# Sums through HBM at the turn between two passes, a gate chain moved to the last pairs, and a shorter head of the mix

## The chip, the core and the metric

The kernel runs on one core of one Trainium2 chip. The metric is the device time of one execution in microseconds (us). Five engines work side by side, each with a queue of its own: PE (matmuls; it adds up in eight banks), DVE and ACT (element-wise work and evacuation of the banks), POOL, and SP, which issues the DMAs in the order in which they are written. HBM is the memory outside the core.

## The reference

One layer of a hybrid encoder over a prompt of 2048 tokens and a sample of 64, width 1024:

```
mod = c @ w_mod + b_mod; shift, scale, gate = split(mod, 3)
h = rmsnorm(x, norm_in_w) * (1 + scale) + shift
b_gate, c_gate, h_a, g_a, z, xbc_raw, dt_raw = split(h @ w_in)
u = c_gate * h_a
y_a = gated_rmsnorm(b_gate * causal_dwconv(u), g_a)
x, B, C = split(silu(causal_dwconv(xbc_raw)))
y = ssd_chunked(x, softplus(dt_raw), a, B, C) + d_skip * x      # the scan over time
y_b = gated_rmsnorm(y, z)
out = rmsnorm(x + gate * (concat(y_a, y_b) @ w_out))
```

Outputs are out for prompt and sample, and the states of the convolutions and of the scan.

## The kernel before

All products are made in pairs of rounded parts: a float32 tensor is split into a rounded high part (ACT casts, `split` L170) and the rest as a low part (DVE subtracts, L171), and a product is three matmuls, high by high, high by low, low by high.

`phase_project` computes h @ w_in by a scheme of seven products instead of eight on 2 × 2 blocks. The second input dimension and the tokens are halved, so the input h of a pass stands as blocks A11, A12, A21, A22, and the seven products read A11, S1, S2, S4, S3, A12, A22, where S1 = A21 + A22, S2 = S1 − A11, S4 = A12 − S2 and S3 = A11 − A21. A *pair* g is two tiles of 128 columns of w_in. Pairs 0 to 27 go over the first pass (tokens 0 to 1023, matmuls 512 wide), pairs 28 to 55 over the second (tokens 1024 to 2111, the sample among them; two units 272 wide). The kinds are z pairs, pairs of x, B and C (`raw_row`), and a pairs in groups of four: c, h, g and b. Pair 22 is an h pair, 25 to 31 are z pairs, 52 to 55 are c, h, g and b.

The main loop goes over pairs 2 to 54 and, in each, over the seven products s. Each step issues, in this order: the matmuls of product (g, s) (`product`, L275); the weights' high part of a later product (`w_hi`, ACT, L241); the hooks that are written down for (g, s); background work that fits (taps of the convolutions, L432); the weights' low part (`w_lo`, DVE, L232, with subtractions of weight quarters in place, `raw<-raw`); and `evac`. `evac` copies products 0, 1 and 2 to `keep` (ACT, L300), adds keep to products 3, 4 and 5 (DVE, L308), and copies product 6 (ACT, L306). Products 0, 2, 4 and 6 accumulate in one bank, 1 and 3 in another. So product 2 can't start before the copy of product 0 to keep is done, and the same holds two products further on each time. Engines run what they got in order, so what stands ahead of an evacuation in the order of the code delays PE.

The input of the second pass is prepared in hooks. Before, x is loaded in two groups of four chunks of 128 rows (pairs 24 to 26), normalized, transposed and stored to `hs_d` in HBM. From pair 27 on, `second_in` loads blocks of it (`t_a`), and seven hooks `second(s)` make the sums (L849 and L232) and their splits, one after each product, into the places that the products of pair 27 have just left. Other hooks: `load_state`, `turn_state`, `sample_x` and `sample_h` for the sample; `gate_load` and `gate_part`, eight parts of the product of c with the gate's third of w_mod. The last part adds b_mod in four quarters (`gb`, L628): SP loads a quarter of b_mod, DVE adds the bank, SP stores it, in turns through one tile.

After pair 54 `last_pair` computes the last pair as plain products into all eight banks (L1146), and prepares the mix meanwhile: `split_wo` splits sixteen tiles of w_out (ACT L1234, DVE L1235) that SP loads as `wo_raw` into tiles that come free (`homes`); `decay` computes the scan's decays of the first chunk (ACT, L1257 and L1258); `evac_last` evacuates the banks (L482). `phase_mix` then goes over 17 chunks; its first matmuls (`sd`, L1295) use banks of the last pair. Its head splits the rest of w_out.

## Time and profile before

| | |
|---|---|
| median of 3 runs | 1800.84 us (1800.67 to 1802.07) |
| profiled execution | 1800.68 us |
| its span, first to last instruction | 1798.9 us |
| mean granted clock of PE | 0.987 |
| PE, DVE, ACT busy | 1721.1, 1308.4, 824.8 us |
| HBM read, written | 158.74, 49.69 MB |

The profile is of one execution. An instruction's row gives its start from the beginning of the span, its duration, engine, line and operation, out<-in, how many were grouped (x), and in brackets the idle time of its engine before it and what ended it. Rows of groups end with the busy time, the mean ns of one, and the idle time before. "PEclk" is the clock that PE was granted, 1.00 being full speed.

### The profile page before, as it was taken

Reading aid. Unit: us, or ns where it says so; the run is one execution under the profiler, and the core shown is the slowest. Engines: PE = TensorE matmul, PEld = TensorE weight load, DVE = VectorE, ACT = ScalarE, POOL = GpSimd, SP = SyncE. Lnnn points to the kernel's source line nnn. Section 1 sums busy time; section 2 is a strip of 40 time slices with the busy share of each in tenths; the row PEclk is TensorE's granted clock in tenths of the full one; section 3 lists DMA queues with packets and bytes.
Section 4 is the critical chain, followed back from the end, with each engine's and each line's share of the span. In section 5 each row is a group of like instructions: output and inputs, shape, how many; then the busy total and the mean of one; then the engine's idle time right before and its main releaser. Section 6 shows DMA issues by size and latency. Waiting matters only on the chain.

```text
span 1798.9 us, 26916 instructions
## 1 busy us (share of the span) xinstructions
PE 1721.1 (96%) x10561; PEld 1512.7 (84%) x10561; DVE 1308.4 (73%) x2015; ACT 824.8 (46%) x1559; POOL 101.8 (6%) x222
## 2 busy tenths in 40 slices
...
GB/s 333 70 88 76 96 104 82 95 118 78 110 129 186 195 109 85 100 73 73 80 103 89 87 78 96 83 84 109 217 146 167 108 173 107 170 111 170 112 147 35
DMA packets 181826, 210.17 MB, mean 117 GB/s; under 512 B 21012, under 2 KB 147972, under 8 KB 181700
## 3 DMA queue, kind: packets, MB, share of 16 engines
...
HBM read 158.74 MB, written 49.69 MB: 116 GB/s over the span
## 4 chain that ended last, share of the span: by engine, by line
PE 83%; DVE 6%; ACT 4%; DMA 4%; issue 2%; SPq 0%; POOL 0%; POOLq 0%; ACTq 0%; DVEq 0%
PE bank L275 53%; PE mm L1398 13%; PE mm L1405 6%; PE sd L1323 2%; PE sd L1327 2%; PE sd L1329 2%; DMA t_a<-hs_d 1%; PE sd L1295 1%; PE sd L1299 1%; PE bank L1025 1%; DMA rb<-r_d 1%; DVE w L232 1%; DVE xt L208 1%; DMA wo_raw<-in_w_out_dram 1%; DMA hs_d<-h_g 1%
## 5 line engine op out<-in xcount | busy, mean ns | idle before, releaser
L275 PE MATMUL bank<-hiS,w 128*128 128x272 f32 (+1 forms) x2560 | 600.9, 324 | 13.9 <-ACT keep L300 13.7
L275 PEld LDWEIGHTS bank<-hiS,w 128*128 128x128 f32 x2560 | 432.7, 189 | 52.7 <-ACT keep L300 18.2
L275 PE MATMUL bank<-hiA,w 128*128 128x272 f32 (+1 forms) x1920 | 452.9, 324 | 20.8 <-DVE z_row L308 9.8
L275 PE MATMUL bank<-loS,w 128*128 128x272 f32 (+1 forms) x1280 | 413.3, 323 | 0.0
L275 PEld LDWEIGHTS bank<-hiA,w 128*128 128x128 f32 x1920 | 325.8, 190 | 50.3 <-DVE z_row L308 10.8
L232 DVE TENSOR_TENSOR w<-raw,w 128x512 fp32r<-128x512 f32 x318 | 217.8, 688 | 173.2 <-ACT w L241 158.8
L241 ACT CAST w<-raw 128x512 fp32r<-128x512 f32 x318 | 196.2, 622 | 255.1 <-PE bank L275 135.3
L275 PE MATMUL bank<-loA,w 128*128 128x272 f32 (+1 forms) x960 | 310.5, 323 | 0.0
L275 PEld LDWEIGHTS bank<-loS,w 128*128 128x128 f32 x1280 | 242.3, 189 | 15.9
L275 PEld LDWEIGHTS bank<-loA,w 128*128 128x128 f32 x960 | 182.0, 190 | 12.2
L300 ACT COPY keep<-bank 128x272 f32<-128x272 f32 (+1 forms) x240 | 106.2, 450 | 137.9 <-PE bank L275 137.4
L381 DVE SCALAR_TENSOR_TENSOR acc<-raw_row,par,acc 128x1024 f32<-128x1024 f32 (+1 forms) x96 | 126.4, 1317 | 2.0
L232 DVE TENSOR_TENSOR raw<-raw 128x512 f32<-128x512 f32 x161 | 111.0, 689 | 3.7
L1398 PE MATMUL mm<-woh,vah 128*128 128x512 f32 (+1 forms) x272 | 109.5, 403 | 0.0
L1398 PE MATMUL mm<-woh,vbh 128*128 128x512 f32 (+1 forms) x272 | 109.2, 401 | 0.0
L1398 PE MATMUL mm<-wol,vah 128*128 128x512 f32 (+1 forms) x272 | 106.5, 392 | 0.0
L1398 PE MATMUL mm<-wol,vbh 128*128 128x512 f32 (+1 forms) x272 | 106.1, 390 | 0.0
L1257 ACT ACTIVATE lt<-rb,acum 128x128 f32<-128x128 f32 x256 | 78.3, 388 | 6.0 <-DMA rb<-r_d 5.2
L1405 PE MATMUL mm<-woh,vbh 128*128 128x512 f32 (+1 forms) x272 | 67.2, 390 | 0.0
L1405 PE MATMUL mm<-woh,vah 128*128 128x512 f32 (+1 forms) x272 | 67.2, 389 | 0.0
L241 ACT CAST w<-t 128x512 fp32r<-128x512 f32 x53 | 32.7, 618 | 75.0 <-PE bank L275 75.0
L1423 ACT ACTIVATE t<-xr 128x512 f32<-128x512 f32 (+1 forms) x34 | 21.5, 632 | 92.8 <-DVE xr L1422 92.8
...
## 6 DMA issues: line engine op xcount, KB each, us to landing
...
```

What stands on the lines that cost most here:

```text
L232: DVE.tensor_tensor(out=out, in0=a, in1=b, op=ALU.subtract)
L241: ACT.copy(out=w[:, 0], in_=w_src(g, j))
L275: PE.matmul(ps[:, 0:n], w[:, a, k, :], h[:, k, o:o + n], start=(s in (0, 1, 5) and k == 0 and i == 0), stop=(k == 3 and i == 2), skip_grou ...
L300: ACT.copy(out=keep[s][:, o:o + n], in_=b["y" if s == 1 else "x"][:, 0:n])
L381: DVE.scalar_tensor_tensor(out=acc[:, 0:n], in0=r[:, k:k + n], scalar=cb_w(k, t), in1=acc[:, 0:n], op0=ALU.mult, op1=ALU.add)
L1257: ACT.activation(out=lt[:, h, :], in_=rb[:, h, :], func=AF.Relu, scale=-1.0, bias=acum[:, c, h0 + h:h0 + h + 1])
L1323: PE.matmul(py4[64 * e:64 * e + 64, j, :], xd[:, 2 * j + e, :], lt[:, 2 * j + e, :], start=True, stop=True)
L1327: PE.matmul(po4[:, j, :], state[:, hf, j * 128:(j + 1) * 128], xb[:, 6 + j // 2, :], start=True, stop=True)
L1329: PE.matmul(ps[:, g * 256:(g + 1) * 256], bc[:, g, :], xe[:, 4 * g:4 * g + 4, :].rearrange("p h q -> p (h q)"), start=True, stop=True)
L1398: PE.matmul(ps[:n], hl[:, 0, k, 0:n], wo[k0 + k][i][:, nn * 512:(nn + 1) * 512], start=(k == 0 and i == 0), stop=False)
L1405: PE.matmul(ps[:n], hl[:, 1, k, 0:n], wo[k0 + k][0][:, nn * 512:(nn + 1) * 512], start=False, stop=(k == 7))
L1423: ACT.activation(out=t[:n], in_=xr[:n, s], func=AF.Square, accum_out=ss[:n, nn:nn + 1])
```

## The change

1. The second pass's input is loaded in four groups of two chunks from pair 19 on; four transposes of 128 × 128, two per input tile, go to one bank ahead of its two copies. In pairs 23 to 25 the blocks are loaded (`h_q`), the eight adds are made there, and the four sums are stored to a new tensor `hq_d` in HBM. From pair 26 on the inputs of the products are loaded ready made (`t_q`), three ahead, and pairs 27 and 28 only split them; for products 2 and 3 the splits are written behind the evacuation of their step (`behind`).
2. State and sample hooks go from pairs 22 and 23 to 18 and 19, the gate's parts from pairs 18 to 22 to pairs 51 to 53.
3. In `last_pair` the banks are numbered anew, the first chunk's decays are loaded straight into their tiles and computed behind the first two weight splits, nine splits of w_out are made rather than twelve, and the evacuations stand behind the sixth and the ninth. The head of the mix splits seven rather than four.

DVE around the middle of pair 27, where the splits of S4 and S3 stand (`w2` to `w4` are weight parts of pair 28, `z_row` evacuations; the order of before first):

```order
L232 TENSOR_TENSOR w2_4675<-raw_4400,w2_4675 128x512
L308 TENSOR_TENSOR z_row_4644<-bank2_4602,keep2_4661 128x512
L232 TENSOR_TENSOR t_a21_4591<-t_a12_4649,t_a21_4591 128x1088
L232 TENSOR_TENSOR t_a21_4593<-t_a12_4651,t_a21_4593 128x1088
L171 TENSOR_TENSOR loS4_4704<-t_a21_4591,hiS4_4703 128x1088
L171 TENSOR_TENSOR loS4_4704<-t_a21_4593,hiS4_4703 128x1088
L232 TENSOR_TENSOR w3_4699<-raw_4400,w3_4699 128x512
L308 TENSOR_TENSOR z_row_4644<-bank1_4570,keep1_4629 128x512
L232 TENSOR_TENSOR t_a11_4587<-t_a11_4587,t_a21_4728 128x1088
```

```order
L233 TENSOR_TENSOR w2_4674<-raw_4473,w2_4674 128x512
L309 TENSOR_TENSOR z_row_4645<-bank2_4599,keep2_4660 128x512
L233 TENSOR_TENSOR w3_4690<-raw_4473,w3_4690 128x512
L309 TENSOR_TENSOR z_row_4645<-bank1_4579,keep1_4630 128x512
L172 TENSOR_TENSOR loS2_4695<-t_q_4503,hiS2_4694 128x1088
L172 TENSOR_TENSOR loS2_4695<-t_q_4505,hiS2_4694 128x1088
L233 TENSOR_TENSOR w4_4719<-t3_4627,w4_4719 128x512
L309 TENSOR_TENSOR z_row_4644<-bank3_4704,keep0_4597 128x512
L172 TENSOR_TENSOR loS4_4724<-t_q_4622,hiS4_4723 128x1088
L172 TENSOR_TENSOR loS4_4724<-t_q_4624,hiS4_4723 128x1088
```

Between the evacuations of z_row stood two adds and two splits; now the first two evacuations have only a weight part between them, and the third stands ahead of the splits of S4.

DVE at the end of pair 53, an h pair (`u_row` its evacuations, L432 and L433 taps, `w5` and `w6` weight parts of pair 54, `raw` the subtraction that ACT's cast for `w6` reads):

```order
L232 TENSOR_TENSOR w4_11136<-t3_11008,w4_11136 128x512
L308 TENSOR_TENSOR u_row_11038<-bank2_11110,keep0_10974 128x272
L308 TENSOR_TENSOR u_row_11038<-bank3_11111,keep0_10974 128x272
L432 SCALAR_TENSOR_TENSOR c_row_10816<-u_row_11041,par_70,c_row_10816 128x1090
L232 TENSOR_TENSOR w5_11171<-raw_10780,w5_11171 128x512
L232 TENSOR_TENSOR raw_10780<-raw_10780 128x4x128
L418 TENSOR_TENSOR u_row_11038<-u_row_11038,c_row_10815 128x1024
L420 TENSOR_TENSOR u_row_11038<-u_row_11038,c_row_10815 128x64
```

```order
L233 TENSOR_TENSOR w4_11174<-t3_11036,w4_11174 128x512
L309 TENSOR_TENSOR u_row_11066<-bank2_11148,keep0_11000 128x272
L309 TENSOR_TENSOR u_row_11066<-bank3_11149,keep0_11000 128x272
L629 TENSOR_TENSOR gb_11215<-bank5_10711,gb_11215 2x256 x4
L433 SCALAR_TENSOR_TENSOR c_row_10824<-u_row_11069,par_71,c_row_10824 128x1090
L233 TENSOR_TENSOR w5_11209<-raw_10784,w5_11209 128x512
L233 TENSOR_TENSOR raw_10784<-raw_10784 128x4x128
L419 TENSOR_TENSOR u_row_11066<-u_row_11066,c_row_10823 128x1024
```

The gate's four adds now stand ahead of the tap, the weight part and the subtraction. Before, they stood in pair 22 in the like place.

ACT in the last pair (`woh` high parts of w_out, `lt` the decays):

```order
L1234 ACTIVATE woh0_11627<-wo_raw_11659,par_70 128x1024
L1234 ACTIVATE woh1_11629<-wo_raw_11661,par_70 128x1024
L1234 ACTIVATE woh2_11631<-wo_raw_11663,par_70 128x1024
L1234 ACTIVATE woh3_11633<-wo_raw_11621,par_70 128x1024
L1234 ACTIVATE woh4_11635<-wo_raw_11622,par_70 128x1024
L1257 ACTIVATE lt_11683<-rb_11619,acum_78 128x128 x8
L1258 ACT_TABLE_LOAD
L1258 ACTIVATE lt_11683<-lt_11683 128x1024
L1234 ACTIVATE woh5_11637<-wo_raw_11669,par_70 128x1024
L1234 ACTIVATE woh6_11657<-wo_raw_11673,par_70 128x1024
L1257 ACTIVATE lt_11706<-rb_11695,acum_78 128x128 x8
L1258 ACTIVATE lt_11706<-lt_11706 128x1024
```

```order
L1266 ACTIVATE woh0_11680<-wo_raw_11712,par_71 128x1024
L1187 ACTIVATE lt_11672<-lt_11672,acum_79 128x128 x8
L1189 ACT_TABLE_LOAD
L1189 ACTIVATE lt_11672<-lt_11672 128x1024
L1266 ACTIVATE woh1_11682<-wo_raw_11715,par_71 128x1024
L1187 ACTIVATE lt_11673<-lt_11673,acum_79 128x128 x8
L1189 ACTIVATE lt_11673<-lt_11673 128x1024
L1266 ACTIVATE woh2_11684<-wo_raw_11718,par_71 128x1024
L1266 ACTIVATE woh3_11686<-wo_raw_11720,par_71 128x1024
L1266 ACTIVATE woh4_11688<-wo_raw_11727,par_71 128x1024
L1266 ACTIVATE woh5_11690<-wo_raw_11740,par_71 128x1024
L1266 ACTIVATE woh6_11710<-wo_raw_11753,par_71 128x1024
```

The two decays went from behind the fifth and seventh cast to behind the first and second.

The diff, cut:

```diff
+    hq_d = dram.tile([4, 128, 4, 544], F32, tag="hq_d", name="hq_d")
...
+        def hook_at(t, fn):
+            hook(t // 7, t % 7, fn)
+
         for k in range(8):
-            hook(18 + k // 2, 1 + 3 * (k % 2), lambda k=k: gate_load(k, 2 + k % 2))
-            hook(18 + k // 2 + (k % 2), 6 if k % 2 == 0 else 2, lambda k=k: gate_part(k))
+            hook_at(51 * 7 + 3 + 2 * k, lambda k=k: gate_load(k, 2 + k % 2))
+            hook_at(51 * 7 + 6 + 2 * k, lambda k=k: gate_part(k))
...
-        hook(22, 3, load_state)
-        hook(23, 1, turn_state)
+        hook(18, 6, load_state)
+        hook(19, 3, turn_state)
...
-        hook(22, 5, sample_x)
-        hook(23, 0, lambda: x_scale(xin["s"], xin["ss"]))
-        hook(23, 2, sample_h)
+        hook(18, 0, sample_x)
+        hook(18, 4, lambda: x_scale(xin["s"], xin["ss"]))
+        hook(18, 6, sample_h)
 
         def group_load(gi):
-            xin[gi] = load_rows(range(8 + 4 * gi, 12 + 4 * gi), range(2, 6))
+            xin[gi] = load_rows(range(8 + 2 * gi, 10 + 2 * gi), (2, 3))
             xin[gi, "ss"] = x_ss()
 
         def group_turn(gi, j):
...
-            o = row(6 + j % 2, [128, 2, 512], "h_g")
+            o = row(4 + j, [128, 4, 256], "h_g")
+            for i in range(0, 4, 2):
+                pt = bank()
+                for e in range(2):
+                    k = 4 * j + i + e
+                    for off, n, t in xin[gi]:
+                        PE.transpose(pt[:, 256 * e + off:256 * e + off + n], t[:n, k * 128:(k + 1) * 128], ident[:n, :n])
+                for e in range(2):
+                    k = 4 * j + i + e
+                    ACT.activation(out=o[:, i + e, :], in_=pt[:, 256 * e:256 * e + 256], func=AF.Identity,
+                                   scale=scol[:, k, 0:1], bias=bcol[:, k, 0:1])
+            store_h(o, 4 * j, 256 * gi, 256)
+        for gi in range(4):
+            t0 = 19 * 7 + 1 + 8 * gi
+            hook_at(t0, lambda gi=gi: group_load(gi))
             for i in range(2):
-                k = 2 * j + i
-                pt = turn_x(xin[gi], k)
-                ACT.activation(out=o[:, i, :], in_=pt, func=AF.Identity, scale=scol[:, k, 0:1], bias=bcol[:, k, 0:1])
-            store_h(o, 2 * j, 512 * gi, 512)
-
-        for gi, (gl, gt) in enumerate(((24 * 7, 25 * 7), (25 * 7 + 4, 26 * 7 + 3))):
-            hook(gl // 7, gl % 7, lambda gi=gi: group_load(gi))
+                hook_at(t0 + 3 + i, lambda gi=gi, i=i: x_sums(xin[gi], xin[gi, "ss"], i, i + 1))
+            hook_at(t0 + 5, lambda gi=gi: x_scale(xin[gi], xin[gi, "ss"]))
+            for j in range(2):
+                hook_at(t0 + 6 + 2 * j, lambda gi=gi, j=j: group_turn(gi, j))
+
+
+        blocks = {}
+
+        def sums_in(i):
+            for n, (k0, o) in enumerate(((0, 0), (0, 544), (4, 0), (4, 544))):
+                t = row(2 + n, [128, 2, 544], "h_q")
+                SP.dma_start(out=t, in_=hs_d[:, k0 + 2 * i:k0 + 2 * i + 2, o:o + 544])
+                blocks[n] = t
+
+        def sums_step(i, n):
+            a11, a21, a12, a22 = (blocks[x] for x in range(4))
+            out, x, y, op = ((a22, a21, a22, ALU.add), (a21, a11, a21, ALU.subtract),
+                             (a11, a22, a11, ALU.subtract), (a12, a12, a11, ALU.subtract))[n]
+            DVE.tensor_tensor(out=out, in0=x, in1=y, op=op)
+            SP.dma_start(out=hq_d[n, :, 2 * i:2 * i + 2, :], in_=out)
+
+        for i, t0 in enumerate((23 * 7 + 6, 24 * 7 + 5)):
+            hook_at(t0, lambda i=i: sums_in(i))
+            for n in range(4):
+                hook_at(t0 + 3 + n, lambda i=i, n=n: sums_step(i, n))
+
+        tm = {}
+        SOURCE = {"A11": (hs_d, 0, 0), "A12": (hs_d, 4, 0), "A22": (hs_d, 4, 544),
+                  "S1": (hq_d[0], 0, 0), "S3": (hq_d[1], 0, 0), "S2": (hq_d[2], 0, 0), "S4": (hq_d[3], 0, 0)}
+
+        def second_in(j, r):
+            src, k0, o = SOURCE[PRODS[j]]
+            tm[j] = []
             for i in range(2):
-                hook((gt - 3 + i) // 7, (gt - 3 + i) % 7, lambda gi=gi, i=i: x_sums(xin[gi], xin[gi, "ss"], 2 * i, 2 * i + 2))
-            hook((gt - 1) // 7, (gt - 1) % 7, lambda gi=gi: x_scale(xin[gi], xin[gi, "ss"]))
-            for j in range(4):
-                hook((gt + j) // 7, (gt + j) % 7, lambda gi=gi, j=j: group_turn(gi, j))
-
-        def temp(r, name, k0, o):
-            ts = []
-            for i in range(2):
-                t = row(r + i, [128, 2, 544], name)
-                SP.dma_start(out=t, in_=hs_d[:, k0 + 2 * i:k0 + 2 * i + 2, o:o + 544])
-                ts.append(t)
-            return ts
-
-        tm = {}
-
-        def second_in():
...
-        def second(s):
-            a, b, c = tm["a"], tm["b"], tm.get("c")
-            if s == 1:
-                for i in range(2):
-                    DVE.tensor_tensor(out=b[i], in0=b[i], in1=c[i], op=ALU.add)
-                tm["c"] = temp(6, "t_a12", 4, 0)
...
-            q = PRODS[s]
-            put(q, {"A11": tm["a"], "S1": b, "S2": b, "S4": b, "S3": a, "A12": c, "A22": tm["b"]}[q])
-
-        hook(27, 0, second_in)
-        for s in range(7):
-            hook((27 * 7 + s + 1) // 7, (s + 1) % 7, lambda s=s: second(s))
+                t = row(r + i, [128, 2, 544], "t_q")
+                SP.dma_start(out=t, in_=src[:, k0 + 2 * i:k0 + 2 * i + 2, o:o + 544])
+                tm[j].append(t)
+
+        def second(j):
+            hi, lo = h_tile(PRODS[j], 544)
+            for i, t in enumerate(tm.pop(j)):
+                split(t, hi[:, 2 * i:2 * i + 2, :], lo[:, 2 * i:2 * i + 2, :])
+            if j + 3 < 7:
+                second_in(j + 3, (6, 2, 4)[j % 3])
+
+        hook(26, 0, lambda: second_in(0, 6))
+        hook(26, 1, lambda: second_in(1, 2))
+        hook(26, 2, lambda: second_in(2, 4))
+        behind = {}
+        for j, t, late in ((0, 1, 0), (1, 2, 0), (2, 4, 1), (3, 5, 1), (4, 6, 0), (5, 7, 0), (6, 9, 0)):
+            if late:
+                behind[27, t] = lambda j=j: second(j)
+            else:
+                hook_at(27 * 7 + t, lambda j=j: second(j))
 
...
-            pss = {(f, h): [bank(2 * (f + 2 * h) + u) for u in range(2)] for h in range(2) for f in range(2)}
+            pss = {fh: [bank(no + u) for u in range(2)] for fh, no in (((0, 1), 4), ((1, 1), 2), ((0, 0), 0), ((1, 0), 6))}
...
+            fast = [p1.tile([128, 8, 128], F32, tag="lt", name="lt", bufs=2) for _ in range(2)]
+            p1.tile([128, 8, 128], F32, tag="rb", name="rb_")
+            xbs = [p1.tile([128, 8, 128], F32, tag="xb", name="xb", bufs=2) for _ in range(2)]
...
-            homes = ["w6", "row6", "row7", None, None, "w6", "row6", "row7", "w6", "row6", "row7", "w6"]
+            homes = ["w6", "rb", "row6", "row7", "w6", "rb", "row6", "row7", "w6"]
...
+            def load_decay(hf):
+                SP.dma_start(out=fast[hf], in_=r_d[hf * 8:hf * 8 + 8, :].partition_broadcast(128))
+
+            def decay_first(hf):
+                for h in range(8):
+                    ACT.activation(out=fast[hf][:, h, :], in_=fast[hf][:, h, :], func=AF.Relu, scale=-1.0,
+                                   bias=acum[:, 0, 8 * hf + h:8 * hf + h + 1])
+                ACT.activation(out=fast[hf], in_=fast[hf], func=AF.Exp, scale=-1.0)
+                held[0, hf] = fast[hf]
...
-            for k in range(5):
-                load_o(k)
-            for k in range(12):
+            load_o(0)
+            load_decay(0)
+            load_o(1)
+            load_decay(1)
+            load_o(2)
+            load_o(3)
+            for hf in range(2):
+                SP.dma_start(out=xbs[hf], in_=xb_d[0, :, hf])
+                loads[0, hf] = [xbs[hf], None]
+            SP.dma_start(out=va[:, 0:6, :], in_=va_d[16, :, 0:6, 0:NS_TOK])
+            for k in range(9):
                 split_wo(k, raw_o.pop(k))
-                if k + 5 < 8 or 5 <= k <= 8:
-                    load_o(k + 5 if k < 3 else k + 3)
-                if k == 4:
-                    decay(0, 0)
-                    prefetch(0, 1)
-                    SP.dma_start(out=va[:, 0:6, :], in_=va_d[16, :, 0:6, 0:NS_TOK])
-                if k == 6:
-                    decay(0, 1)
-                if k == 8:
+                if k + 4 < 9:
+                    load_o(k + 4)
+                if k < 2:
+                    decay_first(k)
+                elif k == 5:
                     evac_last(1, True)
                     evac_last(1, False)
             evac_last(0, False)
...
                 evac(p, g, s)
+                if (g, s) in behind:
+                    behind[g, s]()
...
-        for k, tag, bufs in ((12, "xr", 2), (13, "xr", 2), (14, "gate", 1), (15, "nf", 1)):
+
+        def load_o(k, tag, bufs):
             raw_o[k] = sp.tile([128, D], F32, tag=tag, name="wo_raw", bufs=bufs)
             SP.dma_start(out=raw_o[k], in_=w_out[k * 128:(k + 1) * 128, :])
+
+        for k, tag, bufs in ((9, "xr", 2), (10, "xr", 2), (11, "gate", 1), (12, "nf", 1)):
...
-        for k in (12, 13):
+        for k, nxt, tag, bufs in ((9, 13, "xr", 2), (10, 14, "xr", 2), (11, 15, "gate", 1), (12, None, "", 0)):
             split_wo(k, raw_o[k])
+            if nxt:
+                load_o(nxt, tag, bufs)
         join1(0, 0)
         ssd1(0, 1)
         join2(0, 0)
         prefetch(1, 0)
-        for k in (14, 15):
+        for k in (13, 14, 15):
```

25 lines of the change are left out of this document (2 added, 23 removed).

## The prediction, made before the changed kernel was run

> **What bounds the kernel now.** I read the page first, then the waits of PE, then the stretches in which PE stands, and last the rows at their edges.
>
> ```profile
> PE 1721.1 (96%) x10561; PEld 1512.7 (84%) x10561; DVE 1308.4 (73%) x2015; ACT 824.8 (46%) x1559; POOL 101.8 (6%) x222
> ```
>
> PE bounds it, and both kernels issue the same PE work. So the change can only win time in which PE stands (1798.9 − 1721.1 = 77.8 us) or runs at half clock. Who holds PE up:
>
> ```profile
> PE bank L275 <- ACT keep L300: 13.7, 8, 3.5
> PE sd L1295 <- DVE c_row L482: 11.0, 1, 11.0
> PE bank L275 <- DVE z_row L308: 9.8, 3, 6.8
> PE bank L275 <- ACT z_row L306: 7.8, 1, 7.8
> PE bank L275 <- DVE u_row L308: 2.8, 1, 2.8
> ```
>
> (Columns: total us, times, longest.) These are evacuations that come late; nearly all lie at the turn between the passes (pairs 22 to 28) and once at the head of the mix (L1295). The stretches, with PE's busy time first, the granted clock behind POOL, then the DMA's share and GB/s:
>
> ```profile
> 482.50:673.10 190.60, 158.63 (x764) 130.74 (x761) 114.57 (x157) 92.98 (x164) 2.93 (x5) 0.93 0.47 152
> 530.30:599.60 69.30, 66.05 (x317) 53.60 (x316) 37.55 (x58) 42.92 (x84) 2.02 (x2) 1.00 0.52 167
> 599.60:673.10 73.50, 49.49 (x255) 43.10 (x254) 45.75 (x54) 33.39 (x46) 0.00 (x0) 0.84 0.47 156
> 1243.50:1281.30 37.80, 26.79 (x205) 26.57 (x205) 21.72 (x28) 25.28 (x39) 0.00 (x0) 0.87 0.63 210
> ...
> 503.70:507.10 3.40, 3.40 (x10) 2.62 (x9) 3.26 (x5) 1.95 (x5) 0.18 (x1) 0.50 0.04 8
> 521.95:525.35 3.40, 3.40 (x15) 2.81 (x16) 2.23 (x4) 0.98 (x2) 0.00 (x0) 1.00 0.76 214
> 657.30:660.70 3.40, 3.40 (x17) 3.40 (x16) 2.68 (x6) 1.18 (x4) 0.00 (x0) 0.50 0.40 94
> 1271.70:1281.90 10.20, 3.11 (x12) 2.75 (x13) 8.20 (x16) 3.70 (x5) 0.00 (x0) 0.50 0.47 149
> ```
>
> In pairs 22 to 28 (482.5 to 673.1) PE stands 190.60 − 158.63 = 32.0 us, 24.0 of them in pairs 27 and 28 (73.50 − 49.49). The mean clock there is 0.93. Full speed alternates with half speed, so half speed lasts (1 − 0.93) × 2 × 190.6 = 27 us: eight stretches of 3.4 us between the rows 503.70 and 657.30. PE is busy 20.6 us of these, and work at half clock takes twice its time, so 10.3 us are lost. **The ceiling of the turn is 32.0 + 10.3 = 42.3 us.** What brings half clock on:
>
> ```profile
> 502.78 0.50 PE L275 MATMUL bank<-hiA,w 128*128 128x512 f32 x1 [2.83 <-DVE u_row L308]
> 521.95 0.50 PE L275 MATMUL bank<-hiS,w 128*128 128x512 f32 x1 [1.88 <-ACT keep L300]
> 632.87 0.80 PE L275 MATMUL bank<-hiA,w 128*128 128x512 f32 x1 [6.83 <-DVE z_row L308]
> ```
>
> Behind the gap of 2.83 us stands a stretch at 0.50 (503.70), behind that of 1.88 us one at 1.00 (521.95). I count a loss of 1.7 us (half of a busy 3.4) for each new gap of 2.8 us or more, and half of that, 0.8, for one between 1.9 and 2.8. The Trainium skill ("TensorE: Matmul & The Clock Gate", Part 1: The HAM clock gate) has the clock drop when a whole activity window of about 3.4 us was idle. By that rule no gap under 3.4 us costs clock and my sum would come out some 3 us lower; the trace's 2.83 us gap disagrees, and I go by the trace.
>
> **The change, part by part.** *The turn.* Of the old pairs 27 and 28 these rows show what DVE does:
>
> ```profile
> L171 DVE TENSOR_TENSOR loS<-t_a,hiS 128x1088 fp32r<-128x1088 f32 x8 | 10.1, 1289 | 0.0
> L232 DVE TENSOR_TENSOR t_a<-t_a,t_a 128x1088 f32<-128x1088 f32 x6 | 7.6, 1287 | 7.4 <-DMA t_a<-hs_d 7.4
> 629.11 2.49 DVE L171 TENSOR_TENSOR loS<-t_a,hiS 128x1088 fp32r<-128x1088 f32 x2
> 631.52 0.69 DVE L232 TENSOR_TENSOR w<-raw,w 128x512 fp32r<-128x512 f32 x1
> 632.13 0.68 DVE L308 TENSOR_TENSOR z_row<-bank,keep 128x512 f32<-128x512 f32 x1
> 638.85 1.29 DVE L232 TENSOR_TENSOR t_a<-t_a,t_a 128x1088 f32<-128x1088 f32 x1 [6.04 <-DMA t_a<-hs_d]
> ...
> 603.82 0.39 PE L275 MATMUL bank<-hiS,w 128*128 128x512 f32 x1
> 607.67 0.39 PE L275 MATMUL bank<-hiS,w 128*128 128x512 f32 x1
> ```
>
> PE's 6.83 us gap ends with the z_row evacuation of 632.13, which stood behind two adds, two splits and a weight part. After the change the eight adds (8 × 1.29 = 10.3 us) and their DMA waits (7.4 us) are gone from here, and the evacuations of z_row stand ahead of the splits of S2 and S4. What is left between the first split and the last product of pair 27 is 12 splits and, by the order above, 14 weight parts and evacuations. Back to back they take 1.24 and 0.61 (the spacing of rows 629.11 to 632.13): 12 × 1.24 + 14 × 0.61 = 23.4 us. The seven products of pair 27 need 7 × 2.72 = 19.0 (between the last two rows are 17 matmuls in a piece, 3.85 / 17 = 0.2265 each, and a product has twelve). So DVE falls 4.4 us behind, and PE must stand about that long: the lower bound. I walked the queue of each engine by these durations: gaps of 1.4 and 2.25 us at the end of pair 27, and 1.45, 0.45 and 0.95 in pair 28, where ACT's hi casts and DVE's first subtraction of the next weights wait on one another; 6.5 us, and 0.8 of clock. I take 7.3 (4.4 to 14; the upper end adds one more gap like the old one of 6.83).
>
> *The adds in their new place.* The eight adds go to pairs 23 to 25, each between a load of 557 KB from HBM and a store to it. DVE has room: 37.6 busy of 69.3 us in pairs 24 to 26. DMA too, on average: 16 × 0.557 = 8.9 MB more, with what stays some 13 MB in 46 us, or 280 GB/s, where row 521.95 has 214 at a share of 0.76. What is tight is time: a block's load is issued one product after the store of the last turned rows, and its first add stands three products later, 8.2 us. A load like that at 638.85 came 6.0 us after its evacuation. By my walk the loads land 1.3 to 1.8 us ahead of the adds; I take 0.5 us of new stall. Bounds: nothing, or 14 us (at each of two block groups 3.5 to 5.3 us late, with 1.7 of clock). The Trainium skill ("DMA: Bandwidth & Descriptors", Anatomy of one DMA) speaks against these hops: about 2.0 us fixed for each transfer, most of it the receipt of a write, longest into HBM. By its fit a store and the load behind it would take an estimated 6.6 us; that is inside 8.2, so by it the term would be zero, and the sum 0.5 lower.
>
> *State, sample and gate out of pairs 18 to 23.* The state and sample parts go to pairs 18 and 19, where PE stands nowhere now; I count nothing: PE has weights of two pairs loaded as cover; without it one gap like the 2.83 would be the price. The gate's chain leaves pair 22:
>
> ```profile
> 490.93 0.62 PE L620 MATMUL bank<-raw_gate,cvec 128*2 128x256 f32 x8
> 491.62 0.41 DVE L628 TENSOR_TENSOR gb<-bank,gb 2x256 f32<-2x256 f32 x1 [2.80 <-PE bank L620]
> 497.61 0.43 DVE L628 TENSOR_TENSOR gb<-bank,gb 2x256 f32<-2x256 f32 x1 [1.60 <-DMA gb<-in_b_mod_dram]
> 499.45 1.14 ACT L241 CAST w<-raw 128x512 fp32r<-128x512 f32 x2 [7.78 <-DVE raw L232]
> ```
>
> Four adds, each waiting for its own small load, hold DVE from 491.62 to 498.04, three periods of 2.0 us and one add; ACT's cast waits behind for the subtracted weights, 7.78 us, and from that comes the old gap of 2.83 at 502.78 (part of the ceiling). Now the chain stands behind product 6 of pair 53:
>
> ```profile
> 1225.53 0.29 PE L275 MATMUL bank<-hiS,w 128*128 128x272 f32 x1
> 1243.57 0.29 PE L1146 MATMUL bank<-hiS,w 128*128 128x272 f32 x1
> ...
> 1228.67 1.35 DVE L432 SCALAR_TENSOR_TENSOR c_row<-u_row,par,c_row 128x1090 f32<-128x1090 f32 x1
> 1225.28 0.84 ACT L300 COPY keep<-bank 128x272 f32<-128x272 f32 x2
> ```
>
> From 1225.53 (product 1 of pair 54) to 1243.57 (the last pair) are six products of 3.007, so product 0 starts at 1222.5. The gate's matmuls come first: 1223.1. DVE then needs 3 × 2.0 + 0.43 for the chain: 1229.6; by the order above, a tap (1.27), a weight part (0.61) and the subtraction (0.60) come next: 1232.1; ACT's cast of that (0.6): 1232.7; and only behind it the copy to keep of product 0 (0.39): 1233.1. It was done at 1225.7 before. Product 2 accumulates into that bank and is due at 1222.5 + 0.62 + 2 × 3.007 = 1229.1. PE stands 4.0 us, and 1.7 of clock follow: **+5.7** (2 if the small loads are quicker in this quiet stretch; 8 if they take 2.8 us). The turning of x in pieces of 256 rather than 512 columns makes 32 ACT copies of 16, at most 16 × 0.42 = 6.7 us more (1225.28 has two of 272 in 0.84); ACT had 26.4 us free in pairs 24 to 26 alone (69.3 − 42.9), so I count nothing, and with that cover gone a gap of about one copy.
>
> *The last pair.*
>
> ```profile
> 1278.79 1.01 PE L1295 MATMUL sd<-xb 128*128 128x128 f32 x3 [11.01 <-DVE c_row L482]
> 1243.77 12.23 SPq L1164 DMA_DIRECT2D wo_raw<-in_w_out_dram  x8
> 1251.89 5.00 ACT L1234 ACTIVATE woh<-wo_raw,par 128x1024 fp32r<-128x1024 f32 x4 [3.38 <-DMA wo_raw<-in_w_out_dram]
> 1256.96 2.45 ACT L1257 ACTIVATE lt<-rb,acum 128x128 f32<-128x128 f32 x8
> 1274.23 1.15 ACT L1234 ACTIVATE woh<-wo_raw,par 128x1024 fp32r<-128x1024 f32 x1 [3.04 <-DMA wo_raw<-in_w_out_dram]
> 1292.06 2.48 DVE L1235 SCALAR_TENSOR_TENSOR wol<-wo_raw,par,woh 128x1024 fp32r<-128x1024 f32 x2 [2.42 <-ACT woh L1234]
> 1297.16 1.26 PE L1323 MATMUL sd<-lt,xd 128*64 128x128 f32 x16 [0.88 <-DVE lt L1309]
> ```
>
> PE's products end 11.0 us before 1278.79, at 1267.8; it waits for the evacuation behind twelve weight splits. The stretch 1271.70 to 1281.90 is at half clock, of which PE's own 3.1 us lose 1.5. Now nine splits stand ahead. What limits them is the loads: nine of weights, two of decays and two of xb, 13 × 0.524 = 6.8 MB, at the 350 GB/s that such bursts have here 19.5 us from 1243.8, to 1263.3, and some 2.5 us until the last has been split; then the evacuation, 1.5. With the hold-ups of the homes (the row 1243.77 shows SP blocked 12.23 us for them) I put PE's restart at 1269.8 rather than 1278.8: −9.0, and −1.5 of clock. Given back: the head of the mix splits seven rather than four, and four, not two, stand ahead of the first join. That is 2 × 1.24 on DVE at least, and with ACT's 2 × 1.1 ahead of it 4.7 at most; I take 3.3, near the middle since ACT can run ahead by one, so the gap of 0.88 becomes 4.2, and 1.7 of clock follow. **Net −5.5**, between −9 (the extra splits hide under the mix's matmuls) and −1 (the loads keep their old pace, as the wait of 3.04 at 1274.23 suggests they can).
>
> **Sum.** −42.3 + 7.3 + 0.5 + 5.7 − 5.5 = −34.3. The profiled execution took 1800.68 (span 1798.9 and 1.8 around it), 0.16 under the median of 1800.84, so the forecast is 1766 (1800.68 − 34.3 = 1766.4).
>
> **Rivals.** (1) The sums' loads come late: 5 us at each of two groups rather than 0.5 in all, +9.5: 1776. For it: the 6.04 wait of 638.85 behind an evacuation's store. Against: three products of distance. (2) The gate's chain is covered: −5.7, 1760; for it the quiet queues at pair 53, against it 499.45, where the same chain delayed ACT 7.78 us. (3) The last pair gives its gain back in the mix's head: +5.5, 1772. (4) The change doesn't do what it says: the evacuations stay late at the turn, because each z_row waits for its keep, which waits on ACT behind casts that wait for DVE; a third of the 42.3 − 7.8 counted as won remains, +11.5: 1778. (5) The other side, slower: SP issues all DMAs in order, and each sum's store stands in SP until its add is done, with the next block's loads and the weights behind it, as SP stood 12.23 us at 1243.77. If each of the eight steps then costs a full 6.0 us round trip, +48: 1814. It decides from (1804.4 − 1766) / 8 = 4.8 us a step; against it, weights are loaded two pairs ahead, about 38 us.
>
> **How the numbers follow.** Likeliest, 1766: 0.45, by itself 1759 to 1772. (1) 0.15, (2) 0.12, (3) 0.13, (4) 0.10, (5) 0.03, anything else 0.02. From 1755 to 1780 all but (5), the rest and the tails are in, 8 in 10. A measurement of this kernel tells 0.2%, 3.6 us, from no change. Faster 0.95: all but (5) and a mixture of (1), (3) and (4) at once; same 0.02, slower 0.03.
>
> **What would show it.** PE's waits on z_row gone or under 3 us in pairs 27 and 28; no DVE wait over 1 us on a load of h_q; a wait of about 4 us on keep at product 2 of pair 54, followed by a stretch at 0.50; PE's wait at the first sd matmul of the mix 2 to 3 us, and one of about 4 us ahead of its second group. I am wrong if pairs 19 to 25 show PE gaps over 2 us, if the turn keeps over 15 us, or if the gate's four adds come at a spacing other than 2.0 us.

## The result, and the profile after

The changed kernel took 1771.07 us, median of four runs (1769.35 to 1774.05), against 1800.76 of the kernel before. The ratio is 0.984, with a 95% interval of 0.9821 to 0.9859: about 29 us faster. The forecast was 1766, in a range of 1755 to 1780. The profiled execution took 1769.35, 3 us more than was forecast for it; it is the fastest of the four, and the median lies 5 us above the forecast. Its page begins:

```profile
span 1767.5 us, 26974 instructions
PE 1716.4 (97%) x10561; PEld 1512.3 (86%) x10561; DVE 1306.8 (74%) x2019; ACT 826.9 (47%) x1575; POOL 102.5 (6%) x224
```

The span is 31.4 us shorter, PE busy 4.7 us less (fewer matmuls at half clock), and PE stands 51.1 us where it stood 77.8. The waits of PE (total us, times, longest; lines have moved, by one in the loop and by 32 in the mix):

```profile
PE bank L214 <- DVE xt L209: 14.0, 5, 13.1
PE bank L276 <- ACT keep L301: 9.5, 6, 4.1
PE sd L1327 <- DVE c_row L483: 3.8, 1, 3.8
PE sd L1355 <- DVE lt L1341: 3.3, 1, 3.3
...
PE bank L276 <- DVE z_row L309: 2.4, 3, 1.2
PE bank L276 <- ACT z_row L307: 2.0, 1, 2.0
PE bank L276 <- DVE b_row L309: 1.0, 1, 1.0
```

The first row, which the prediction's list leaves out, is nearly all the wait for x at the start of the program, which the change does not touch (16.3 before). Before, PE waited 13.7 us for keep, 11.0 for c_row, and 9.8 and 7.8 for the evacuations of z_row by DVE and by ACT. The row of u_row (2.8) is gone; that of lt (1.8 in two waits before) is larger, that of b_row is new. The stretches (PE's busy time first, the granted clock behind POOL):

```profile
482.20:633.20 151.00, 142.79 (x706) 120.30 (x705) 106.29 (x144) 78.53 (x132) 1.84 (x6) 0.99 0.63 212
524.20:585.40 61.20, 58.00 (x253) 47.05 (x252) 40.67 (x55) 22.86 (x37) 0.00 (x0) 1.00 0.88 302
585.40:633.20 47.80, 42.82 (x254) 38.44 (x254) 35.12 (x46) 30.87 (x44) 0.00 (x0) 0.96 0.57 183
...
611.46:614.87 3.41, 3.41 (x17) 3.41 (x17) 1.69 (x4) 1.81 (x3) 0.00 (x0) 0.50 1.08 390
1198.56:1201.97 3.41, 3.31 (x14) 3.31 (x15) 3.34 (x6) 2.07 (x7) 0.32 (x2) 0.50 0.02 5
1242.93:1246.34 3.41, 3.03 (x12) 2.75 (x13) 2.88 (x7) 0.90 (x2) 0.00 (x0) 0.50 0.53 147
1263.41:1270.24 6.83, 6.21 (x26) 4.33 (x27) 6.83 (x10) 4.58 (x5) 0.00 (x0) 0.50 0.74 253
```

Pairs 22 to 28 take 151.0 us instead of 190.6, and PE stands 8.2 us in them instead of 32.0 (4.97 in pairs 27 and 28, 24.0 before). Their half-clock stretches went from eight to one. The price of it is in the last two columns: the DMA is busy 0.88 of pairs 24 to 26, at 302 GB/s, where it was 0.52 and 167.

The gaps that are left, each with what ended it:

```profile
557.27 0.50 PE L276 MATMUL bank<-hiS,w 128*128 128x512 f32 x1 [1.94 <-ACT keep L301]
609.95 0.39 PE L276 MATMUL bank<-hiA,w 128*128 128x272 f32 x1 [2.00 <-ACT z_row L307]
1198.66 0.59 PE L276 MATMUL bank<-hiS,w 128*128 128x272 f32 x1 [4.12 <-ACT keep L301]
1243.31 1.22 PE L1327 MATMUL sd<-xb 128*128 128x128 f32 x4 [3.82 <-DVE c_row L483]
1264.03 1.98 PE L1355 MATMUL sd<-lt,xd 128*64 128x128 f32 x16 [3.28 <-DVE lt L1341]
```

They stand at the sums, at the end of pair 27, at product 2 of pair 54, at the mix's first matmuls and ahead of its second group. What DVE and ACT do behind two of them:

```profile
534.08 1.29 DVE L849 TENSOR_TENSOR h_q<-h_q 128x1088 f32<-128x1088 f32 x1 [4.02 <-DMA h_q<-hs_d]
552.81 1.29 DVE L849 TENSOR_TENSOR h_q<-h_q 128x1088 f32<-128x1088 f32 x1 [4.82 <-DMA h_q<-hs_d]
...
1188.39 0.41 DVE L629 TENSOR_TENSOR gb<-bank,gb 2x256 f32<-2x256 f32 x1 [1.98 <-PE bank L621]
1190.41 0.42 DVE L629 TENSOR_TENSOR gb<-bank,gb 2x256 f32<-2x256 f32 x1 [1.60 <-DMA gb<-in_b_mod_dram]
1197.70 0.62 ACT L242 CAST w<-raw 128x512 fp32r<-128x512 f32 x1 [9.44 <-DVE raw L233]
```

The first add of each block group waits 4 to 5 us for its load. The gate's adds come 2.02 us apart, and ACT's cast waits 9.44 us behind them; the keep copy that PE needs follows it.

### The profile page after: what moved, and what is told of

Same layout as the page of the kernel before. It is cut to its first block, busy times and chain, and to the rows that moved or that the text cites. A ratio compares the mean times of both kernels' runs of the same rounds, so it can differ in the third digit from the quotient of the medians.

```text
span 1767.5 us, 26974 instructions
## 1 busy us (share of the span) xinstructions
PE 1716.4 (97%) x10561; PEld 1512.3 (86%) x10561; DVE 1306.8 (74%) x2019; ACT 826.9 (47%) x1575; POOL 102.5 (6%) x224
## 4 chain that ended last, share of the span: by engine, by line
PE 86%; DVE 5%; DMA 4%; ACT 3%; issue 2%; SPq 0%; POOL 0%; POOLq 0%; DVEq 0%; ACTq 0%
PE bank L276 54%; PE mm L1430 14%; PE mm L1437 7%; PE sd L1355 2%; PE sd L1359 2%; PE sd L1361 2%; PE sd L1327 1%; DMA h_q<-hs_d 1%; PE sd L1331 1%; DMA praw<-in_w_mod_dram 1%; PE bank L1041 1%; DVE w L233 1%; DMA hq_d<-h_q 0%; DMA xt<-in_x_prompt_dram 0%; PE bank L530 0%
## 5 line engine op out<-in xcount | busy, mean ns | idle before, releaser
L1289 ACT ACTIVATE lt<-rb,acum 128x128 f32<-128x128 f32 x240 | 73.4, 388 | 3.5 <-DMA rb<-r_d 3.1
```

What stands on the lines that cost most here:

```text
L1289: ACT.activation(out=lt[:, h, :], in_=rb[:, h, :], func=AF.Relu, scale=-1.0, bias=acum[:, c, h0 + h:h0 + h + 1])
```

## The experiments

Twelve kernels were run. "Less" and "more" below are against the changed kernel unless something else is named; ratios are to the kernel before, with their 95% intervals. The kernel before, run again beside these kernels, had medians of 1799.0 to 1801.1 us, so a difference between two medians is good to about 2 us; for what a place is worth, the lengths of the pairs in the profiles are better (most are taken from the second product of one pair to that of the next).

**The adds put back into the turn.** Does PE stand at the turn because DVE has too much to do there, or because the data came late?

```diff
-            for i, t in enumerate(tm.pop(j)):
+            ts = tm.pop(j)
+            if PRODS[j][0] == "S":
+                for t in ts:
+                    DVE.tensor_tensor(out=t, in0=t, in1=t, op=ALU.max)
+            for i, t in enumerate(ts):
                 split(t, hi[:, 2 * i:2 * i + 2, :], lo[:, 2 * i:2 * i + 2, :])
```

> Changed kernel with eight DVE operations of 128 x 1088 put back into the turn, ahead of the splits of S1, S2, S4 and S3: max(t, t) on the loaded inputs, which changes nothing in the values. Theory (in pair 27 DVE is the bound, and its excess over PE is what PE waits): DVE had 4.4 us more work than PE there, so all 8 x 1.25 = 10 us fall on PE, plus two or three stretches at half clock of 1.7: +10 to +15, 1780 to 1784. Rival (the gain of the turn came from the loads being there in time, not from the adds): +3 at most, 1772.

Measured: 1780.11 us, ratio 0.9892 (0.9877 to 0.9906), 9.0 more. Between the starts of pairs 26 and 29 the loss is 8.3 us; the rest of the profiled execution's 10.7 is in the sums and the start. Two rows of PE:

```profile
602.13 0.50 PE L276 MATMUL bank<-hiS,w 128*128 128x512 f32 x1 [2.52 <-ACT keep L301]
622.55 0.59 PE L276 MATMUL bank<-hiA,w 128*128 128x272 f32 x1 [10.42 <-ACT z_row L307]
```

The inputs are there in time and the sums are ready made, yet a gap of 10.42 us is back in the place of the old 7.75, for nothing but eight operations of DVE. That is the theory's mechanism, a little under its size (8.3 of 10 to 15): some of the 10 us fell into time in which DVE waited (its idle time in pairs 27 and 28 went from 12.54 to 11.05 us).

**The splits ahead of the evacuations.** The last column of the table of hooks, `late`, set to 0:

```diff
-        for j, t, late in ((0, 1, 0), (1, 2, 0), (2, 4, 1), (3, 5, 1), (4, 6, 0), (5, 7, 0), (6, 9, 0)):
+        for j, t, late in ((0, 1, 0), (1, 2, 0), (2, 4, 0), (3, 5, 0), (4, 6, 0), (5, 7, 0), (6, 9, 0)):
```

> Changed kernel, but the splits of S2 and S4 stand ahead of the evacuations of their steps again, as in the old order; the adds stay away. Theory (DVE's total over pair 27 sets most of it, the order of evacuation and split the rest): each of two evacuations comes 2.5 us later, PE's gaps at the end of pair 27 grow by 2 to 5 us and one more stretch at half clock follows: +2 to +5, 1771.5 to 1774.5. Rival (only DVE's total counts): 1769.4 within 1. Second rival (the order is what won the turn): more than +8.

Measured: 1774.9 us, 0.9864 (0.9849 to 0.9878), 3.8 more; 3.0 of it between pairs 26 and 29 (pair 27 alone 2.7). The profile has a new gap in pair 27:

```profile
608.51 0.50 PE L276 MATMUL bank<-hiA,w 128*128 128x512 f32 x1 [2.42 <-DVE z_row L309]
```

So order is worth 3 us, the adds 8: two causes in one turn, both as the theory had them. The forecast stretch at half clock did not follow: pairs 27 and 28 have none here, where the changed kernel's profile has one. Together the two are 11.3 of the 25.6 us by which pairs 27 and 28 became shorter (73.7 to 48.1). The other 14 us no run isolates. Before, ACT and DVE waited there 15.5 us for loads of the blocks (`t_a`), now 1.7 for the ready sums (`t_q`):

```profile
  DMA t_a<-hs_d: 15.5, 7
  DMA t_q<-hq_d: 1.7, 1
```

That fits, but no kernel here brings the late loads back by themselves.

**The blocks of h_q in the order of use.** The first add needs the second and the fourth block that were loaded.

```diff
-            for n, (k0, o) in enumerate(((0, 0), (0, 544), (4, 0), (4, 544))):
+            for n, (k0, o) in ((1, (0, 544)), (3, (4, 544)), (0, (0, 0)), (2, (4, 0))):
```

> Changed kernel, but the four blocks of h_q are loaded in the order in which the adds use them (the first add's two blocks first). Theory (the loads come late because the first add needs the last of four loads, 2.2 MB): DVE's two waits of 4.02 and 4.82 us on h_q shrink by about two loads, 3 us each, PE's gaps of 0.98 and 1.94 in pairs 24 and 25 go: -2.9, 1766.5. Rival (what is late is the store of the turned rows ahead of the loads, so all four loads are late): the waits stay within 1 us, 1769.

Measured: 1765.79 us, 0.9812 (0.9798 to 0.9827), 5.3 less. DVE's wait on the first block fell from 4.02 to 0.90 us, and the two together from 8.8 to 2.2:

```profile
531.39 1.29 DVE L849 TENSOR_TENSOR h_q<-h_q 128x1088 f32<-128x1088 f32 x1 [0.90 <-DMA h_q<-hs_d]
```

PE has no gap left in pairs 24 and 25, and they take 38.1 us instead of 42.2, 4.1 less. Order of the loads, and not the store ahead of them, was what made them late. The second gap at this place also varied: from 1.94 to 3.80 us in the eight profiled executions with the old order of loads (those of the changed kernel and of seven kernels below and above); in the four with the new order there was none. The two pairs take 42.2 to 45.5 us in the eight, and the changed kernel's profile is the one at 42.2.

**The gate's small loads ahead of its adds.**

```diff
-                for j in range(4):
-                    q, col = slice(32 * j, 32 * j + 2), slice(j * 256, (j + 1) * 256)
+                quarters = [(slice(32 * j, 32 * j + 2), slice(j * 256, (j + 1) * 256)) for j in range(4)]
+                for j, (q, col) in enumerate(quarters):
                     SP.dma_start(out=gb[q, 0:256], in_=b_mod[:, 2 * D + j * 256:2 * D + (j + 1) * 256]
                                  .partition_broadcast(2).rearrange("p o n -> p (o n)"))
+                for q, col in quarters:
                     DVE.tensor_tensor(out=gb[q, 0:256], in0=ps[q, 0:256], in1=gb[q, 0:256], op=ALU.add)
+                for q, col in quarters:
                     SP.dma_start(out=g_d[:, col], in_=gb[q, 0:256])
```

> Changed kernel, but the four small loads of b_mod are written ahead of the gate's four adds, the four stores behind them. Theory (SP's order makes the chain: each load stands behind the store of the quarter ahead, and that behind its add): the adds come back to back, 4 x 0.42 = 1.7 us instead of 6.4, the wait of PE at product 2 of pair 54 (4.12 us) goes, and so does the stretch at half clock behind it: 1769.4 - 5.8 = 1763.6 in the profiled execution. Rival (the 2.0 us spacing is the time of one small load whatever stands ahead, or the stall is the matmuls' own): spacing stays 2.0 us, 1769.

Measured: 1764.18 us, 0.9802 (0.9785 to 0.9818), 6.9 less. The adds now stand in one piece:

```profile
1191.98 1.78 DVE L630 TENSOR_TENSOR gb<-bank,gb 2x256 f32<-2x256 f32 x4 [1.98 <-PE bank L621]
```

Pair 54 is 5.86 us shorter, and PE's wait there is gone. (The profiled execution, 1767.55, lost 3.6 of it again in pair 25, at the second loads of h_q, where its gap was 3.80.) The 2.0 us spacing was SP's order, the load of a quarter behind the store of the one ahead.

**The gate's move alone**, in the kernel before:

```diff
-            hook(18 + k // 2, 1 + 3 * (k % 2), lambda k=k: gate_load(k, 2 + k % 2))
-            hook(18 + k // 2 + (k % 2), 6 if k % 2 == 0 else 2, lambda k=k: gate_part(k))
+            tl, tp = 51 * 7 + 3 + 2 * k, 51 * 7 + 6 + 2 * k
+            hook(tl // 7, tl % 7, lambda k=k: gate_load(k, 2 + k % 2))
+            hook(tp // 7, tp % 7, lambda k=k: gate_part(k))
```

> Kernel before, with the gate's eight parts alone moved to pairs 51 to 53. Theory: PE's gap of 2.83 us in pair 22 and the stretch at half clock behind it go (-4.5), and a gap of 4.1 with a stretch at half clock comes at pair 54 (+5.8): +1.3, 1802. Rival (pair 22 keeps a gap of its own without the gate's chain, from the state and sample parts): +5, 1806. Second rival (the late stall is covered by what waits behind it in the last pair): -4, 1796.

Measured: 1801.47 us, ratio 1.0011 (1.0001 to 1.0021): 0.2 to 3.8 us slower than the kernel before. Pair 22 is 5.5 us shorter, pair 54 6.6 us longer. The gap of pair 23, 1.88 us before, stays at 1.83 and now brings a stretch at half clock, so that pair 23 is 1.5 us longer. The gaps of pairs 23 and 54:

```profile
510.52 0.50 PE L275 MATMUL bank<-hiS,w 128*128 128x512 f32 x1 [1.83 <-ACT keep L300]
1226.97 0.60 PE L275 MATMUL bank<-hiS,w 128*128 128x272 f32 x1 [4.11 <-ACT keep L300]
```

Moved alone, the chain wins nothing: its stall goes with it.

**The last pair and the head of the mix as before** (that part of the diff undone).

> Changed kernel with the last pair and the head of the mix as they were before (twelve weight splits, decays between them, four in the head). Theory (traces: restart 7.2 us earlier, 2.4 lost again ahead of the second group of the head, 1.5 more at half clock): +3.3, 1772.7, with PE's gaps back at about 11.0 and 0.9. Rival (the head gives everything back): 1769.4, no change. Second rival (my prediction's size): +5.5, 1774.9.

Measured: 1773.53 us, 0.9855 (0.984 to 0.987), 2.5 more. From the end of the last pair to the end of the program the profiled executions take 531.4 us before, 528.3 after and 530.6 here: that part of the change wins 2.4 to 3.1 us. In the other kernels that have it unaltered, the same stretch takes 527.3 to 528.8 us, so the figure is good to about 1 us.

**The decays late again**, with the nine splits kept:

```diff
-                if k < 2:
-                    decay_first(k)
+                if k in (4, 6):
+                    decay_first(k // 2 - 2)
```

> Changed kernel, with the first chunk's two decays behind the fifth and seventh weight split again; the loads, the nine splits and the evacuations stay. Theory (the loads set the pace of the splits, and ACT makes the decays at the head in time in which it would wait for loads): 7 us of decays then stand among the last splits, where ACT waited 1.86 and 1.52 us for loads, so PE's gap of 3.82 grows by 7 - 3.4 = 3.6, and a stretch at half clock follows: +3.6 to +5.3, 1773 to 1774.7. Rival (twelve splits cut to nine are all of the gain): 1769.4.

Measured: 1776.76 us, 0.9866 (0.9852 to 0.9881), 5.7 more; 4.2 of it behind the last pair (532.4 against 528.3).

```profile
1235.52 1.15 ACT L1266 ACTIVATE woh<-wo_raw,par 128x1024 fp32r<-128x1024 f32 x1 [3.63 <-DMA wo_raw<-in_w_out_dram]
1236.58 2.44 ACT L1187 ACTIVATE lt<-lt,acum 128x128 f32<-128x128 f32 x8
1250.84 1.23 PE L1327 MATMUL sd<-xb 128*128 128x128 f32 x4 [8.22 <-DVE c_row L483]
```

ACT waits 3.63 us for a load and only then begins the decays. With nine splits, seven in the head and the decays late it is no faster than the old twelve and four (530.6). So as far as this run shows, the gain of this part is the early decays; the fewer splits alone win nothing.

**The last evacuation earlier**, behind the seventh split rather than the ninth:

```diff
-            evac_last(0, False)
+                elif k == 6:
+                    evac_last(0, False)
```

> Changed kernel, with the last evacuation of the last pair behind the seventh weight split rather than the ninth. Theory (PE's restart waits for DVE's queue: the last two splits, 2.5 us and 1.3 of waiting for their loads, stand ahead of the evacuation): PE's gap of 3.82 us at the head of the mix shrinks to about 1.6, and one stretch at half clock goes: -2 to -4, 1765.5 to 1767.5. Rival (the two splits are needed next anyway): the gap shrinks, but as much is lost behind it in the head: 1769.

Measured: 1768.46 us, 0.9827 (0.981 to 0.9844), 2.6 less, with runs from 1764.02 to 1772.06. In the profile the gap of 3.82 is gone; PE waits 0.84 us for vah instead:

```profile
1238.32 1.48 DVE L483 TENSOR_TENSOR c_row<-bank,c_row 128x272 f32<-128x272 f32 x4
1239.71 2.47 DVE L1268 SCALAR_TENSOR_TENSOR wol<-wo_raw,par,woh 128x1024 fp32r<-128x1024 f32 x2
1241.02 0.45 PE L1431 MATMUL mm<-woh,vah 128*64 128x512 f32 x1 [0.84 <-ACT vah L1404]
```

Behind the last pair it takes 523.9 us rather than 528.3. By its own runs the median alone would not settle it; the runs with three mends below do.

**Two, not four, splits ahead of the head's first join**, five behind it:

```diff
-        for k, nxt, tag, bufs in ((9, 13, "xr", 2), (10, 14, "xr", 2), (11, 15, "gate", 1), (12, None, "", 0)):
+        for k, nxt, tag, bufs in ((9, 13, "xr", 2), (10, 14, "xr", 2)):
...
-        for k in (13, 14, 15):
+        split_wo(11, raw_o[11])
+        load_o(15, "gate", 1)
+        for k in (12, 13, 14, 15):
```

> Changed kernel, with two of the head's seven weight splits ahead of the first join, as before, and five behind it. Theory (the gap of 3.28 us ahead of the second group and the half clock behind it come from the two extra splits there): the gap goes to 0.9, -2.4 and -1.5: 1765.5. Rival (the seven splits must all be done before the matmuls with vbh: DVE's 2.5 us only move behind the second group): a new gap of 2 to 3 us some 5 us later, 1769.

Measured: 1774.62 us, 0.9852 (0.9837 to 0.9867), 3.6 more. The theory fell, the rival stood:

```profile
1265.84 1.26 PE L1355 MATMUL sd<-lt,xd 128*64 128x128 f32 x16 [0.89 <-DVE lt L1341]
1270.64 0.44 PE L1430 MATMUL mm<-wol,vbh 128*64 128x512 f32 x1 [0.32 <-DVE wol L1267]
1275.54 0.69 PE L1430 MATMUL mm<-wol,vbh 128*64 128x512 f32 x1 [0.87 <-DVE wol L1267]
```

The 3.28 us become 0.89, but five waits of 0.32 to 0.87 us, 3.0 together, follow at the matmuls that use the split weights (the first and the last are shown). The head has that much work of DVE and ACT, wherever it stands. The profiled execution is 5.1 us longer than the changed kernel's, and only 0.8 of that lies behind the last pair; 2.2 lie in pairs 24 and 25, at the loads of h_q, and 1.3 in pair 54.

**The mends together.** Gate and order of loads:

> Changed kernel with both mends: the small loads of b_mod ahead of the gate's adds, and the blocks of h_q loaded in the order of use. Theory (independent places, each worth what its trace showed: 5.9 and 2.9 to 3.6): 1769.4 - 9 = 1760.5. Rival (what one wins, another wait takes): 1764 or more.

Measured: 1759.74 us, 0.9778 (0.9763 to 0.9792). With the earlier evacuation:

> Changed kernel with the small loads ahead of the gate's adds, the blocks of h_q in the order of use, and the last evacuation behind the seventh split. Theory (independent): from 1759.7 (the first two together) less 4.1 (3.0 of gap, the rest clock, by the run with the third alone): 1755.7. Rival: the evacuation's gain is within the spread of that run (1764 to 1772): 1758 to 1760.

Measured: 1755.66 us (1754.86 to 1756.8), 0.9752 (0.9736 to 0.9769). With the head's splits too:

> The three mends, and two rather than four splits ahead of the head's first join. Theory: 1755.7 - 3.9 = 1751.8. Rival (the head's splits only move): 1755.7.

Measured: 1757.52 us, 0.9761 (0.9747 to 0.9776). The mends add up about as their traces said: 11.3 us for two, 15.4 for three, so the earlier evacuation is worth 4.1 here, beyond the spread of these runs (behind the last pair the profile shows 4.2). The fourth costs 1.9. The kernel with three mends is the fastest here, 15 us below the changed one and 45 below the one before.

## Why the prediction was right, point by point

The sum came out at −31.4 in span where −34.3 was forecast, and its terms so:

| term | forecast | measured | from |
|---|---|---|---|
| what stood at the turn goes | −42.3 | −44.0 | what is left: from pair 2 to pair 54 the kernel is 33.6 us shorter, though 6.3 and 4.1 stay |
| stays in pairs 27 and 28 | +7.3 | +6.3 | PE's standing there at full clock |
| the sums' loads | +0.5 | +4.1 | pairs 24 and 25 take 42.2 us, 38.1 with the blocks in order |
| the gate's chain | +5.7 | +5.9 | gap of 4.12, and 1.7 of clock |
| last pair and head | −5.5 | −3.1 | 531.4 to 528.3 behind the last pair |
| sum | −34.3 | −30.8 | span: −31.4 |

The 0.6 us that are left lie ahead of pair 2, where the time differs by 2 us between profiles of the same code (87.9 to 90.0). The forecast was right within its range, and two of its terms were mis-sized, both to the hopeful side: the sums by 3.6 us and the last pair by 2.4. That the turn gave 1.7 more than its ceiling and kept 1.0 less than forecast hid nearly half of that, so the small miss is in part luck. The ceiling counted PE's standing and the clock alone, and a gap can cost more than that: pair 24, at full clock, is 1.27 us longer for a gap of 0.98.

Of the signs that were named, PE's waits on z_row (2.0 at most), the wait of 4 us on keep and the half clock behind it came. DVE's waits on h_q, which were to stay under 1 us, were 4.02 and 4.82. The wait at the first sd matmul was 3.82, not 2 to 3, and that ahead of the second group 3.28, not about 4. Of the signs of being wrong, a gap over 2 us in pairs 19 to 25 was missed by 0.06 us, and five of the seven other kernels with these loads show one (2.27 to 3.80): luck again.

*The turn.* The walk had PE's gaps nearly one by one: 1.4, 2.25, 1.45, 0.45 and 0.95 us. With the blocks of h_q in order they are 1.63, 2.01, 1.30, 0.43 and 0.89, 6.3 us in all. The changed kernel's profile lacks the third, since a stretch at half clock lies there (row 611.46), and yet pairs 26 to 28 take as long (the changed kernel, then the blocks in order):

```profile
568.92:636.03 67.11, 62.13 (x349) 54.95 (x348) 44.78 (x61) 39.35 (x59) 0.00 (x0) 0.97 0.65 212
565.21:632.35 67.14, 60.87 (x350) 53.45 (x349) 44.77 (x61) 39.37 (x59) 0.00 (x0) 1.00 0.65 212
```

All ten kernels that have this turn unaltered take 67.1 us here, the four with a stretch at half clock (5.0 us of standing) and the six without (6.3). So half clock cost nothing here: PE's slower matmuls filled time in which it would have stood, and the 0.8 of clock in the forecast had nothing to price. The lower bound, DVE's 4.4 us above PE's products, left out the waits of ACT and DVE on one another, which the walk had. That DVE's load is one cause of the old standing is shown by the adds put back (8.3), the order's part by the splits ahead of the evacuations (3.0); the other 14 us are open, as said there.

*The gate.* Gap (4.0 forecast, 4.12 measured), spacing (2.0, 2.02) and half-clock stretch came as worked out. The working had them as small loads that each add waits for; the cause is SP's order.

*The sums* were mis-sized, and this is the step that failed: the walk let the loads land 1.3 to 1.8 us ahead of the adds, and DVE waited 4.02 and 4.82 us for them instead. It priced the load by the row at 638.85, one pair of loads behind one store. Here four loads, 2.2 MB together, stand in a row behind a store, the weights' load behind them, at a DMA share of 0.88, and the first add needs the last of the four: from the first load's issue (523.55) to the add (534.08) 10.5 us pass, where the prediction had 8.2 us of room and 6.6 as an estimate for a store and a load. Load order, not the hop through HBM itself, was the cost, as the run with the blocks in order shows: there the hop costs nothing that PE sees. The lateness is that of rival (1), 5 us a group; of DVE's 8.8 us PE felt 4.1, less than half of the rival's price.

*The last pair* was the other mis-sized term. PE's restart has a gap of 3.82, not 2.0: DVE stood on two more splits, for which ACT waited 1.5 us for loads, and the clock's 1.5 that were to be saved there were lost again (row 1242.93). The working took the loads at 350 GB/s. From the start of the last pair to the last cast that waits for a load, the DMA moved 291, and SP was held 11.83 us over five of the loads:

```profile
1215.27:1239.20 23.93, 23.93 (x193) 23.93 (x192) 12.73 (x16) 18.12 (x31) 0.00 (x0) 1.00 0.84 291
1223.75 11.83 SPq L1180 DMA_DIRECT2D wo_raw<-in_w_out_dram  x5
```

The head's gap is 3.28 rather than 4.2, but two stretches at half clock follow it (row 1263.41), not one. Rival (3), that the head gives all back, was too dark: of the 7.2 us won at the restart, 1.5 of gap (lt's waits went from 1.8 to 3.3) and 3.1 of clock are lost again, not all.

*The clock.* Half a price for gaps between 1.9 and 2.8 us fits neither gap at hand. That of 1.94 at 557.27 brought no half clock, that of 2.00 at 609.95 brought a whole stretch, which cost nothing at that place; the last section says why the one did and the other didn't.

## What to carry to other kernels

Where an engine ahead of PE is overbooked in a short stretch, count its work there against PE's: the difference (4.4 us here) is a lower bound of the stall that stays (6.3), and work put back into the stretch costs most of its own length (8.3 of 10 us). The order of that work within the stretch was worth 3.0 us. An order written by hand must be right in the DMA's queue too: a load behind a store that waits for an add made four adds of 0.4 us last 6.5, and four blocks loaded in another order than that of use cost 4.1 us and more. Work that is moved whole takes its stall along; look at what stands behind it on the new place. And a stretch at half clock need not cost time: it took 1.7 us behind the gate's gap, and nothing at the turn, where PE waits for DVE and ACT in any case.

## What the runs showed of the clock

The granted clock changes only at the borders of a grid of 3.413 us that runs through a whole execution, and its phase differs from run to run. What decides is how long PE stood in one field of the grid, not how long a gap is. Fields that follow one another, from three kernels (the gate's move alone, the adds put back, the changed kernel; PE's busy time first, then the clock of the field behind POOL):

```profile
508.33:511.74 3.41, 1.58 (x7) 1.04 (x6) 1.75 (x4) 3.17 (x9) 0.00 (x0) 1.00 0.34 114
511.74:515.15 3.41, 3.41 (x9) 2.65 (x9) 1.29 (x3) 0.00 (x0) 0.00 (x0) 0.50 0.93 235
```

```profile
1204.59:1208.01 3.42, 1.60 (x13) 1.38 (x12) 1.95 (x3) 0.00 (x0) 0.00 (x0) 1.00 0.01 2
1208.01:1211.42 3.41, 1.20 (x9) 1.20 (x10) 3.31 (x6) 2.16 (x6) 0.33 (x2) 1.00 0.00 0
```

```profile
553.43:556.84 3.41, 1.90 (x9) 1.24 (x7) 3.38 (x5) 0.72 (x2) 0.00 (x0) 1.00 1.12 359
556.84:560.25 3.41, 2.98 (x13) 2.46 (x14) 3.41 (x6) 1.53 (x3) 0.00 (x0) 1.00 1.02 382
608.05:611.46 3.41, 1.51 (x12) 1.51 (x13) 3.41 (x4) 2.90 (x4) 0.00 (x0) 1.00 0.97 280
```

In the first fence PE stood 1.83 us in a field, and the next was at 0.50; in the second it stood 1.82 us by the row, 1.80 with the field's borders to the nanosecond, and the next was at 1.00 still. In the third, the gap of 1.94 us at 557.27 is cut by a border: 1.51 us lie in the field at 553.43, and the clock stays; of the gap of 2.00 at 609.95, 1.90 us lie in the field at 608.05, and the next (611.46, above) is at 0.50. Behind the first 45 us the traces of all fourteen kernels agree: at full clock, 1.80 us of standing in a field or less never brought half clock on, 1.83 us or more always did. At the start two traces do not fit: with the splits ahead, a field with 1.97 us of standing was followed by one at 1.00 and the next, with 1.43, by one at 0.50; with two splits ahead of the first join, a field with 1.63 was followed by one at 0.50. What counts there stays open. So behind the start a gap of 2 us brings half clock on when it lies within a field and not when a border cuts it, and one of 3.7 us or more always puts 1.83 us into one of its fields. A stretch at half clock takes about 1.7 us of PE's work, half of a busy 3.4: pair 54 is 5.86 us longer for a gap of 4.12. At the turn, where PE waited for DVE and ACT in any case, it took nothing. The Trainium skill ("TensorE: Matmul & The Clock Gate", Part 1: The HAM clock gate) has the free-running window of 3413 ns, with which the traces agree; that it has to be an idle one as a whole they do not bear out, since a little over half of it was enough (1.83 of 3.41 us).
